# Depthwise convolution of the RG-LRU branch moved into the projections of an S5 / RG-LRU layer on Trainium2

## The chip, the cores and the metric

The kernel runs on one core of one Trainium2 chip. The core has five engines: TensorE (PE, with its weight loads shown as PEld), VectorE (DVE), ScalarE (ACT), GpSimd (POOL) and SyncE (SP, which only issues transfers here). The metric is the device time in microseconds; lower is better. Times of this kernel are medians of repeated executions; the profile is of one execution.

## The reference

One layer of a hybrid backbone, sequence 2048, width 1024, with 256 context tokens in front. All is float32.

```python
z = (rmsnorm(h) * (1 + sc) + sh) @ w_in                  # 1024 -> 4096, tokens and context
u_s5, g_s5, u_lru, g_lru = split(z)                      # 1024 columns each
y_s5  = s5_branch(u_s5, ...)                             # bidirectional state space scan, GLU
xc    = centred_dwconv(u_lru, conv_w) + conv_b           # 4 taps, pad (1, 2), per channel, along time
r, gi = sigmoid(blockdiag(w_a) xc + b_a), sigmoid(blockdiag(w_x) xc + b_x)   # 16 heads of 64, 2 directions
a     = exp(-8 r softplus(-lam));  bx = sqrt(1 - a^2) * (gi * xc)
h     = scan(a, bx)                                      # forward and backward, started from the context's end
out   = rmsnorm(h_in + gate * (concat(y_s5 * silu(g_s5), y_lru * silu(g_lru)) @ w_out))
```

The convolution is depthwise: each channel is the weighted sum of four neighbouring time steps of itself plus a bias. Context and tokens are convolved apart from each other.

## The kernel before

Channels lie on the 128 partitions and time on the free axis. The 1024 channels of a kind are eight blocks of 128, a block of u_lru being one pair of heads. Tokens are four tiles of 512 (0 to 3); the context is one tile of 256 ("c"). Float32 products are made as three passes of a rounded format (`mm3`, L248 to L250, high and low parts), so a tile of 512 columns with a contraction of 1024 takes 24 matmuls.

`projections(half, kinds)` computes a half of the sequence at a time: half 0 has "c", tiles 0 and 1, half 1 has tiles 2 and 3. It is a generator with eight steps a tile. For each block it splits the weights (L240 on ACT, L241 on DVE; half 1 reads split weights back from DRAM at L267), runs the matmuls into one of four PSUM tiles, and evacuates. A u_lru tile is copied by ACT (L313) into a staging tile with two buffers, `st2`, and stored on ACT's queue (L315) to a DRAM tensor `U`; a g_lru tile is activated and stored to `GL`. In half 0 the order is all u_lru blocks, all u_s5, all g_lru, all g_s5, except that the first two u_lru blocks are taken as [c, 0], [c, 0], [1], [1], since tile 1 of the normalised input is still being made.

Beside half 0 runs a side generator, `prepare`, at 0.1375 steps for each projection step: the tables of the S5 branch (`s5_tables`: products on DVE at L602 to L604, transposes on PE at L634, stores on POOL), then the input tiles 2 and 3.

`lru` is a generator beside half 1. On PE the order is the program's (`manual_schedule`, L1112); on the other engines a planner orders by program position among what it thinks ready. For each head pair b it runs `gates` (ten groups of eight small 64x64 matmuls at L397 with one projection step behind each group; half of them read `xc`, half read `xs`, the same data with the two heads exchanged), ACT's sigmoids (L401), then 34 more projection steps during which ACT does tanh, exp and sqrt (L444, L451, L459), DVE multiplies `gi` by `xc` (L447), and the next pair is prepared: `load(b + 1)` reads `U` into `ut` on SP's queue (L372, L373), `conv` makes `xc` with one ACT instruction (L378) and three of DVE (L381) over 2307 columns, and two DMAs on POOL's queue (L385) make `xs`. `ut` and `xs` share one buffer, `xc` has one. `finish(b)` (L407 to L423) does the scans and the product with `GL` on DVE beside the gates of pair b + 1, and stores `YL` on POOL's queue. The first call of `lru` comes after 32 steps of half 1, its first gates 28 steps later.

## Time and profile before

| what | value |
|---|---|
| time, median of 3 runs | 1915.83 us (1912.74 to 1917.07) |
| the profiled execution | 1915.55 us, of which the span is 1913.8 us |
| PE busy | 1728.6 us, 90% of the span |
| DVE / ACT / POOL busy | 1163.8 / 871.7 / 133.1 us |
| mean granted TensorE clock | 0.955 |
| idle of PE before the 259-column gates that read `xs` | 57.4 us |

Matmul records overlap, so PE's busy time says where it idles and not how fast it goes. The granted clock is a share of full speed and stands beside each stretch. The profiled execution agrees with the median within 0.3 us.

The stages of the span are: preparation to 56 us; half 0 from 56 to 544 (u_lru to 213, u_s5 to 344, then g_lru and g_s5); half 1 from 544, with the gates of the eight head pairs from 592 to 1001; then the rest of half 1, the S5 branch, the gated unit and the output projection.

### The profile page before, as it was taken

The numbers are of one execution on the slowest core, as the hardware profiler recorded it, in microseconds if no ns is written. First come the engines' busy times: TensorE is split into PE (matmuls) and PEld (weight loads), VectorE is DVE, ScalarE is ACT, GpSimd is POOL, SyncE is SP. The second block draws the span as 40 slices with busy tenths as digits, with TensorE's granted clock in tenths as the row PEclk, the third lists the DMA queues.
The fourth block names the chain that finished last, engine by engine and source line by source line (L and its number), as shares of the span: only waits on it lengthen the run. The fifth ranks groups of instructions, "written<-read, shape, count | busy, mean of one in ns | idle before, by whom it ended". The sixth has DMA issues, their size and how long they took to land.

```text
span 1913.8 us, 25929 instructions
## 1 busy us (share of the span) xinstructions
PE 1728.6 (90%) x9785; PEld 1370.3 (72%) x9785; DVE 1163.8 (61%) x1950; ACT 871.7 (46%) x1359; POOL 133.1 (7%) x260
## 2 busy tenths in 40 slices
PE   7889999999997887988788996987889999999998
PEld 2676888777874555554456885766878899998886
DVE  5789998741232767576777058999921046435563
ACT  2622232233633666765565887315545534222221
POOL 1012221210000000000000000000000000001111
PEclk9899999999998889998899998998999999999999
DMA  8677787865463456455557877426688766656653
GB/s 264 165 205 267 254 269 227 273 246 166 123 242 121 145 168 195 140 167 178 144 149 218 255 249 231 146 67 201 209 240 264 215 199 197 180 156 204 199 187 86
DMA packets 340207, 373.58 MB, mean 195 GB/s; under 512 B 124413, under 2 KB 276593, under 8 KB 327794
## 3 DMA queue, kind: packets, MB, share of 16 engines
q1 hardware_dynamic: 288176, 233.99, 42.5%
q0 software_dynamic: 19776, 94.92, 14.0%
q10 hardware_dynamic: 32130, 43.01, 6.5%
q8 instruction: 77, 1.26, 0.3%
q14 instruction: 48, 0.39, 0.1%
HBM read 224.05 MB, written 138.35 MB: 189 GB/s over the span
## 4 chain that ended last, share of the span: by engine, by line
PE 57%; DVE 17%; DMA 12%; issue 8%; ACT 4%; SPq 1%; POOL 0%; ACTq 0%; DVEq 0%; POOLq 0%
PE pp L248 9%; PE pp L250 8%; PE pp L249 8%; DVE p L748 4%; PE po L248 4%; PE po L250 4%; PE po L249 4%; PE pg L397 3%; PE pgl L249 3%; PE pgl L248 3%; PE pgl L250 3%; DVE z L749 3%; DVE z L750 3%; DMA xs<-xc 2%; DVE xc L381 2%
## 5 line engine op out<-in xcount | busy, mean ns | idle before, releaser
L248 PE MATMUL pp<-x,w 128*128 128x512 f32 x1024 | 424.2, 414 | 2.1 <-ACT ust L313 2.1
L250 PE MATMUL pp<-x,w 128*128 128x512 f32 x1024 | 407.7, 398 | 2.7 <-DVE w L241 2.7
L249 PE MATMUL pp<-x,w 128*128 128x512 f32 x1024 | 408.0, 398 | 0.2 <-DVE x L213 0.2
L248 PEld LDWEIGHTS pp<-x,w 128*128 128x128 f32 x1024 | 194.4, 190 | 112.1 <-issue 73.2
L250 PEld LDWEIGHTS pp<-x,w 128*128 128x128 f32 x1024 | 194.8, 190 | 47.9 <-DVE w L241 3.5
L249 PEld LDWEIGHTS pp<-x,w 128*128 128x128 f32 x1024 | 195.3, 191 | 36.6 <-issue 0.7
L241 DVE TENSOR_TENSOR w<-wraw,w 128x1024 fp32r<-128x1024 f32 x66 | 80.7, 1222 | 165.2 <-ACT w L240 165.2
L397 PE MATMUL pg<-xs,gw 64*64 64x512 f32 (+1 forms) x320 | 105.0, 646 | 58.4 <-DMA xs<-xc 45.9
L240 ACT CAST w<-wraw 128x1024 fp32r<-128x1024 f32 x66 | 69.2, 1048 | 155.8 <-PE pp L250 123.6
L783 PE MATMUL py<-h,et 128*128 128x128 f32 x512 | 82.4, 286 | 34.9 <-ACT h L776 16.9
L397 PE MATMUL pg<-xc,gw 64*64 64x512 f32 (+1 forms) x320 | 103.1, 636 | 7.9 <-issue 7.3
L250 PE MATMUL po<-x,w 128*128 128x512 f32 x256 | 101.9, 398 | 9.1 <-DVE w L241 9.1
L748 DVE TENSOR_TENSOR p<-z,A 128x128 f32<-128x128 f32 x288 | 104.3, 381 | 5.7
L248 PE MATMUL po<-x,w 128*128 128x512 f32 x256 | 105.4, 412 | 1.0 <-ACT z L727 0.6
L720 PE MATMUL pw<-u,wt 128*128 128x144 f32 x512 | 76.6, 298 | 29.2 <-DMA wt<-WD 21.7
L249 PE MATMUL po<-x,w 128*128 128x512 f32 x256 | 101.7, 397 | 0.7 <-DVE x L814 0.7
L401 ACT ACTIVATE rr<-pg,vcol 128x512 f32<-128x512 f32 (+1 forms) x80 | 51.7, 646 | 106.3 <-PE pg L397 106.3
L248 PE MATMUL po<-ws,yh 128*128 128x512 f32 x256 | 99.6, 389 | 0.0
L249 PE MATMUL po<-ws,yh 128*128 128x512 f32 x256 | 99.6, 389 | 0.0
L250 PE MATMUL po<-ws,yl 128*128 128x512 f32 x256 | 99.6, 389 | 0.0
L720 PEld LDWEIGHTS pw<-u,wt 128*128 128x128 f32 x512 | 72.4, 198 | 37.3 <-ACT z L727 14.5
L783 PEld LDWEIGHTS py<-h,et 128*128 128x128 f32 x512 | 71.0, 201 | 37.2 <-ACT h L776 19.0
(256 smaller groups left out, 3549.0 us busy)
## 6 DMA issues: line engine op xcount, KB each, us to landing
wraw<-in_w_in_dram SPq DMA_DIRECT2D x50, 512.0 KB
WS<-w POOLq DMA_DIRECT2D x24, 1024.0 KB, 7.3
w<-WS SPq DMA_DIRECT2D x24, 1024.0 KB
u<-ZU SPq DMA_DIRECT2D x64, 288.0 KB
ED<-E POOLq DMA_DIRECT2D x16, 1024.0 KB, 6.3
WD<-Wt POOLq DMA_DIRECT2D x32, 512.0 KB, 4.9
wt<-WD SPq DMA_DIRECT2D x32, 512.0 KB
et<-ED SPq DMA_DIRECT2D x32, 512.0 KB
```

The costliest lines, as they stand in the source:

```text
L240: copy(out=w[:, 0], in_=raw)
L241: self.nc.vector.tensor_sub(out=w[:, 1], in0=raw, in1=w[:, 0])
L248: nc.tensor.matmul(ps, lhsT=whi(k), rhs=xhi(k), start=(k == 0), stop=False)
L249: nc.tensor.matmul(ps, lhsT=whi(k), rhs=xlo(k), start=False, stop=False)
L250: nc.tensor.matmul(ps, lhsT=wlo(k), rhs=xhi(k), start=False, stop=(k == KT - 1))
L397: nc.tensor.matmul(pss[w][e * 64:e * 64 + 64, :n], lhsT=gw[ws, d, e, :], rhs=xcs[(w + e) % 2][ws, o:o + n], start=True, stop=True, tile_po ...
L401: nc.scalar.activation(out=dst[:, o:o + n], in_=pss[w][:, :n], func=AF.Sigmoid, bias=bias[w])
L720: nc.tensor.matmul(pw[:, c, :], lhsT=w[:, gi, kt, c, :], rhs=u[:, kt, :], start=(kt == 0), stop=(kt == 1))
L748: v.tensor_mul(out=p, in0=cur.unsqueeze(1).to_broadcast([P, 2, 2, 32]), in1=self.A16[:, :, :, gs])
L749: v.tensor_add(out=nxt, in0=nxt, in1=p[:, 0])
L750: v.tensor_add(out=nxt, in0=nxt, in1=p[:, 1, ::-1])
L783: nc.tensor.matmul(o, lhsT=ms(e[:, i, gi]), rhs=h[:, i, :], start=False, stop=(i == 1))
```

## The change

The convolution leaves `lru` and is done in `projections`, once for the context and once for each half of the tokens. A u_lru tile is copied into a buffer `u` (one buffer, tag `uc`, pool `ucp`) with the padding columns beside it. After tile "c" and after the last tile of the block, `conv` runs one ACT instruction and three of DVE on it into `xcv` (one buffer) and stores the result on POOL's queue into the DRAM tensor `XC`, which takes the place of `U`. Half 0 leaves out the last two columns that need tokens of half 1 and keeps three columns in `halo`; half 1 takes them up, so it convolves 1026 columns, half 0 256 and 1022.

In `lru`, `load` reads `XC` three times on SP's queue: the two 64-row halves into `xs` exchanged, and all rows into `xc`. `xs` and `xc` have a buffer each, and the gate weights `gw` one instead of two. Weights and data of pair b + 1 are asked for after exp in the program, not before tanh. The first four blocks of half 0 are now u_lru [c, 0], g_lru [0], u_lru [1], g_lru [1] of block 0, and the two weight blocks loaded ahead are those.

```diff
--- before.py
+++ after.py
@@ projections @@
         if half == 0:
-            kind, n = kinds[0][0], int(2)
-            blocks[:n] = [(kind, b, ["c", 0]) for b in range(n)] + [(kind, b, [1]) for b in range(n)]
+            blocks.remove(("g_lru", 0, both))
+            blocks[:1] = [("u_lru", 0, ["c", 0]), ("g_lru", 0, [0]), ("u_lru", 0, [1]), ("g_lru", 0, [1])]
...
+            if kind == "u_lru" and tiles[0] != 1:
+                u = self.conv_input(half, b)
...
-                if kind in ("u_lru", "g_lru"):
+                if kind == "u_lru":
+                    pos = 1 if tl == "c" else (3 if half else LC + 4) + tl % 2 * 512
+                    nc.scalar.copy(out=u[:, pos:pos + n], in_=ps[:, :n])
+                    if tl == "c":
+                        self.conv(half, b, u, 0)
+                elif kind == "g_lru":
                     o = self.stp.tile([P, 512], F32, tag="st2", bufs=2, name="ust")
-                    if kind == "u_lru":
-                        nc.scalar.copy(out=o[:, :n], in_=ps[:, :n])
-                        pos = 0 if tl == "c" else LC + tl * 512
-                        nc.scalar.dma_start(out=self.U[r, pos:pos + n], in_=o[:, :n])
...
+            if kind == "u_lru" and tiles[-1] == both[-1]:
+                self.conv(half, b, u)
...
+    def conv_input(self, half, b):
+        nc = self.nc
+        if half == 0:
+            u = self.ucp.tile([P, LC + 4 + 1024], F32, tag="uc", bufs=1, name="uc")
+            nc.gpsimd.memset(u[:, 0:1], 0.0)
+            nc.gpsimd.memset(u[:, LC + 1:LC + 4], 0.0)
+        else:
+            u = self.ucp.tile([P, 1024 + 5], F32, tag="uc", bufs=1, name="uc")
+            nc.gpsimd.memset(u[:, 1027:1029], 0.0)
+            nc.scalar.copy(out=u[:, 0:3], in_=self.halo[:, b, :])
+        return u
+
+    def conv(self, half, b, u, part=1):
+        nc = self.nc
+        cw, cb = self.col["lru_conv_w"], self.col["lru_conv_b"]
+        r = slice(b * P, (b + 1) * P)
+        if half:
+            o, dst, N = 0, LC + 1022, 1026
+        else:
+            o, dst, N = ((0, 0, LC), (LC + 3, LC, 1022))[part]
+        xc = self.ucp.tile([P, 1026 if half else 1024], F32, tag="xcv", bufs=1, name="xcv")[:, :N]
+        nc.scalar.activation(out=xc, in_=u[:, o + 1:o + 1 + N], func=AF.Identity, bias=cb[:, b:b + 1],
+                             scale=cw[:, 8 + b:9 + b])
+        for k in (0, 2, 3):
+            nc.vector.scalar_tensor_tensor(out=xc, in0=u[:, o + k:o + k + N], scalar=cw[:, k * 8 + b:k * 8 + b + 1],
+                                           in1=xc, op0=ALU.mult, op1=ALU.add)
+        nc.gpsimd.dma_start(out=self.XC[r, dst:dst + N], in_=xc)
+        if part and not half:
+            nc.vector.tensor_copy(out=self.halo[:, b, :], in_=u[:, LC + 1025:LC + 1028])
@@ lru @@
-        X0 = LC + 3
-        N = X0 + L
+        N = LC + L
...
-            gw = le.tile([P, 2, 2, 64], F32, tag="gw", bufs=2, name="gw")
+            gw = le.tile([P, 2, 2, 64], F32, tag="gw", bufs=1, name="gw")
...
         def load(b):
-            ut = le.tile([P, N + 3], F32, tag="ut", bufs=1, name="ut")
-            nc.gpsimd.memset(ut[:, 0:1], 0.0)
-            nc.gpsimd.memset(ut[:, LC + 1:LC + 4], 0.0)
-            nc.gpsimd.memset(ut[:, N + 1:N + 3], 0.0)
-            nc.sync.dma_start(out=ut[:, 1:1 + LC], in_=self.U[rows(b), 0:LC])
-            nc.sync.dma_start(out=ut[:, X0 + 1:X0 + 1 + L], in_=self.U[rows(b), LC:])
-            return ut
-
-        def conv(b, ut):
+            xs = big("xs", 1, le)
+            for e in range(2):
+                o = b * P + 64 - e * 64
+                nc.sync.dma_start(out=xs[e * 64:e * 64 + 64, :], in_=self.XC[o:o + 64, :])
             xc = big("xc", 1, le)
-            nc.scalar.activation(out=xc, in_=ut[:, 1:1 + N], func=AF.Identity, bias=cb[:, b:b + 1],
-                                 scale=cw[:, 8 + b:9 + b])
-            for k in (0, 2, 3):
-                v.scalar_tensor_tensor(out=xc, in0=ut[:, k:k + N], scalar=cw[:, k * 8 + b:k * 8 + b + 1],
-                                       in1=xc, op0=ALU.mult, op1=ALU.add)
-            xs = le.tile([P, N + 3], F32, tag="ut", bufs=1, name="xs")
-            for e in range(2):
-                nc.gpsimd.dma_start(out=xs[e * 64:e * 64 + 64, :N], in_=xc[64 - e * 64:128 - e * 64, :])
+            nc.sync.dma_start(out=xc, in_=self.XC[rows(b), :])
             return xc, xs
...
-            if b < 7:
-                gw2, ut = weights(b + 1), load(b + 1)
             for d in range(2):
...
             if b < 7:
-                gw, xcs = gw2, conv(b + 1, ut)
+                gw, xcs = weights(b + 1), load(b + 1)
@@ build @@
-            self.U = dt("U", [D, LC + L])
+            self.XC = dt("XC", [D, LC + L])
...
+                    self.halo = cp.tile([P, 8, 3], F32, name="halo")
                     xa = pool(eA, "xa")
+                    self.ucp = pool(eA, "ucp")
...
-                            self.first = [self.wload(win[:, :, 2 * D + b * P:2 * D + (b + 1) * P]) for b in range(2)]
+                            self.first = [self.wload(win[:, :, k * D:k * D + P]) for k in (2, 3)]
...
                     lru = self.lru(pool(eL, "lp"), pool(eL, "le"))
+                    self.ucp = pool(eL, "ucp1")
```

## Rows read from the trace of the kernel before

**Rows 1.** Windows by stage; the first line names the columns.

```profile
core 0: us, PE busy (x) PEld busy (x) DVE busy (x) ACT busy (x) POOL busy (x), PEclk, DMA share, GB/s
56.40:100.40 44.00, 41.20 (x232) 34.25 (x233) 35.17 (x61) 26.61 (x43) 5.01 (x4) 0.96 0.64 173
100.40:124.00 23.60, 18.29 (x106) 13.43 (x106) 16.47 (x15) 2.60 (x4) 1.08 (x2) 0.86 0.95 219
124.00:213.40 89.40, 86.56 (x570) 67.67 (x569) 85.64 (x112) 25.41 (x48) 22.77 (x33) 1.00 0.67 238
...
280.00:344.10 64.10, 64.10 (x428) 53.13 (x427) 50.95 (x65) 17.32 (x34) 12.72 (x22) 1.00 0.80 237
344.10:410.00 65.90, 65.90 (x390) 52.39 (x389) 50.26 (x64) 20.99 (x35) 13.32 (x23) 1.00 0.75 265
...
592.20:1001.50 409.30, 346.91 (x1592) 200.24 (x1592) 273.32 (x120) 260.80 (x279) 13.27 (x44) 0.89 0.51 154
```

**Rows 2.** Groups, 560 to 1010: xcount, busy us, mean ns, idle before.

```profile
L381 DVE SCALAR_TENSOR_TENSOR xc<-ut,vcol,xc 128x2307 f32<-128x2307 f32 x24 | 62.9, 2620 | 48.7 <-ACT xc L378 48.0
...
L378 ACT ACTIVATE xc<-ut,vcol 128x2307 f32<-128x2307 f32 x8 | 18.5, 2313 | 2.0 <-DMA ut<-U 1.4 <-DMA gw<-in_lru_w_a_dram 0.6
...
L397 PE MATMUL pg<-xs,gw 64*64 64x259 f32 x64 | 22.3, 517 | 57.4 <-DMA xs<-xc 45.9 <-issue 11.5
```

**Rows 3.** PE's timeline: start, us; before the first gates, last gates.

```profile
587.85 0.39 PE L250 MATMUL pp<-x,w 128*128 128x512 f32 x1
...
1000.89 0.59 PE L397 MATMUL pg<-xc,gw 64*64 64x512 f32 x1
```

**Rows 4.** PE's timeline: last gate of pair 0, gates of pair 1.

```profile
620.11 0.59 PE L397 MATMUL pg<-xc,gw 64*64 64x512 f32 x1
...
644.65 0.65 PE L397 MATMUL pg<-xc,gw 64*64 64x259 f32 x2
...
649.17 1.12 PE L397 MATMUL pg<-xs,gw 64*64 64x259 f32 x2 [3.88 <-DMA xs<-xc]
...
658.07 0.64 PE L397 MATMUL pg<-xc,gw 64*64 64x512 f32 x1
...
672.83 0.59 PE L397 MATMUL pg<-xc,gw 64*64 64x512 f32 x1
```

**Rows 5.** Windows of 10 us, gates of pair 1 (columns above).

```profile
650.00:660.00 10.00, 7.83 (x32) 2.82 (x31) 9.93 (x5) 3.03 (x6) 0.00 (x0) 0.63 0.25 72
```

**Rows 6.** Timelines of DVE and POOL between gates of pairs 0, 1.

```profile
624.28 2.56 DVE L447 TENSOR_TENSOR gi<-gi,xc 128x2307 f32<-128x2307 f32 x1 [8.79 <-ACT gi L401]
...
633.09 5.35 DVE L381 SCALAR_TENSOR_TENSOR xc<-ut,vcol,xc 128x2307 f32<-128x2307 f32 x2 [6.25 <-ACT xc L378]
...
644.08 1.02 POOL L385 DMA_DIRECT2D xs<-xc  x2 [23.11 <-DMA w<-WS]
```

**Rows 7.** DMA issues: xcount, KB each, median us to landing.

```profile
WD<-Wt POOLq DMA_DIRECT2D x32, 512.0 KB, 4.9
...
xs<-xc POOLq DMA_DIRECT2D x16, 576.8 KB, 6.9
...
YL<-rr POOLq DMA_DIRECT2D x8, 1024.0 KB, 6.4
...
out_dram<-ot POOLq DMA_DIRECT2D x60, 128.0 KB, 4.7
```

**Rows 8.** Groups: 124 to 213.4, and (last line) 560 to 1010.

```profile
L604 DVE TENSOR_TENSOR E<-E,ot 128x1024 f32<-128x1024 f32 x10 | 12.2, 1219 | 0.0
...
L248 PE MATMUL pp<-x,w 128*128 128x512 f32 x80 | 32.4, 405 | 0.0
...
L167 DVE SCALAR_TENSOR_TENSOR gacc<-wgt,cond,gacc 128x1024 f32<-128x1024 f32 x3 | 3.9, 1285 | 4.9 <-DMA wgt<-in_w_mod_dram 4.8
```

**Rows 9.** SP's waits, 560 to 1010: us in total, times, longest.

```profile
SPq L267 <- PE pp L250: 165.1, 21, 28.4
SPq L420 <- DVE tt L414: 110.9, 6, 22.9
```

More of the change, by code (lines that the diff above doesn't have):

```diff
@@ L309, in projections @@
                         yield
-                if kind in ("u_lru", "g_lru"):
+                if kind == "u_lru":
[4 more added lines that the diff above has]
+                elif kind == "g_lru":
                     o = self.stp.tile([P, 512], F32, tag="st2", bufs=2, name="ust")
-                    if kind == "u_lru":
-                        nc.scalar.copy(out=o[:, :n], in_=ps[:, :n])
-                        pos = 0 if tl == "c" else LC + tl * 512
-                        nc.scalar.dma_start(out=self.U[r, pos:pos + n], in_=o[:, :n])
-                    else:
-                        if half:
-                            nc.scalar.activation(out=o, in_=ps, func=AF.Sigmoid)
-                            nc.vector.tensor_mul(out=o, in0=ps, in1=o)
-                        else:
-                            nc.scalar.activation(out=o, in_=ps, func=AF.Silu)
-                        nc.scalar.dma_start(out=self.GL[r, tl * 512:tl * 512 + 512], in_=o)
+                    if half:
+                        nc.scalar.activation(out=o, in_=ps, func=AF.Sigmoid)
+                        nc.vector.tensor_mul(out=o, in0=ps, in1=o)
+                    else:
+                        nc.scalar.activation(out=o, in_=ps, func=AF.Silu)
+                    nc.scalar.dma_start(out=self.GL[r, tl * 512:tl * 512 + 512], in_=o)
                 elif kind == "u_s5":
@@ L344, in projections @@
                     nc.sync.dma_start(out=self.ZU[kt, r, :, cs], in_=st[:, kt * 8:kt * 8 + 8, :])
+    def conv_input(self, half, b):
[13 more added lines that the diff above has]
+        r = slice(b * P, (b + 1) * P)
+        if half:
+            o, dst, N = 0, LC + 1022, 1026
[10 more added lines that the diff above has]
+            nc.vector.tensor_copy(out=self.halo[:, b, :], in_=u[:, LC + 1025:LC + 1028])
     def lru(self, lp, le):
         nc, v = self.nc, self.nc.vector
-        X0 = LC + 3
-        N = X0 + L
-        tl_x = [(X0 + i * 512, 512) for i in range(4)]
-        cw, cb = self.col["lru_conv_w"], self.col["lru_conv_b"]
-        c_, x_ = slice(0, LC), slice(X0, N)
+        N = LC + L
+        tl_x = [(LC + i * 512, 512) for i in range(4)]
+        c_, x_ = slice(0, LC), slice(LC, N)
         rows = lambda b: slice(b * P, (b + 1) * P)
@@ L391, in gates @@
             bias = [self.col[n][:, d * 8 + b:d * 8 + b + 1] for n in ("lru_b_a", "lru_b_x")]
-            for o, n in [(0, X0)] + (tl_x if d == 0 else tl_x[::-1]):
+            for o, n in [(0, LC)] + (tl_x if d == 0 else tl_x[::-1]):
                 pss = [pool.tile([P, 512], F32, tag=tag, name="pg") for pool, tag in ((self.psG, "g"), (self.psT, "t"))]
@@ L426, in lru @@
         gw = weights(0)
-        xcs = conv(0, load(0))
+        xcs = load(0)
         yield 28
```

## Prediction

> **What bounds the kernel now.** I read three views in this order: the busy shares by stage, the waits of TensorE in the stage that the change is about, and then DVE in the stage that gets the new work.
>
> By stage, PE is busy without a break in the later part of half 0, where it alone sets the time. Two stretches are different [rows 1]. From 592 to 1001 us, the gates of the eight head pairs, PE is busy 347 of 409 us at a granted clock of 0.89: this is the worst stretch of the first half. From 124 to 213 us, the u_lru blocks of half 0, PE is busy 86.6 of 89.4 us, but DVE is busy 85.6: there the two are nearly level, and DVE has no room.
>
> In the gates the chain of one pair can be followed [rows 4, 6]. The last gate of pair 0 ends at 620.7 (620.11 + 0.59). PE then runs 34 projection steps until the first gate of pair 1 at 644.65, which is 23.95 us. The gates that read `xs` start only at 649.17, after an idle time that ended with the DMA from `xc` to `xs`. That DMA was issued at 644.08, because the convolution stands before it: DVE's first two products started at 633.09. Over all pairs PE idles 57.4 us before the short gates that read `xs`, most of it for that DMA [rows 2]. The idle time costs twice: between 650 and 660 the granted clock is 0.63, so part of the stretch ran at the lower level (1.2 GHz instead of 2.4), right after PE had idled [rows 5]. The first gates of pair 1 took 1.12 us for a pair of 259 columns; later ones take 0.64 us for 512 columns [rows 4].
>
> **Part by part: the gates.** Removed per pair are one ACT instruction of 2.31 us and three of DVE of 2.62 us [rows 2], and the transfer of `xs` behind them. What is left of the chain is a load. Its parts, after the gates end at G: `gw` and `xs` may be issued at G, since their buffers come free then; `xc` may be issued when the second product L447 has read the old one. In pair 0 that is 624.28 + 2.56 = 626.8, or G + 6.1 [rows 6]. No row shows these reads, so I bound them by the nearest ones: one transfer of 1024 KB took 6.4 us and one of 577 KB 6.9 us [rows 7]. If the three overlap, `xc` ends last, at G + 6.1 + 6.4 = G + 12.5. If they follow each other, it is 6.9 + 6.9 + 6.4 = 20.2, so G + 20.2. PE arrives at G + 23.95. Both ends are ahead of it, so I let the wait vanish, with a margin of 3.8 to 11.5 us.
>
> The row of 577 KB has 64 partitions a transfer, the one of 1024 KB has 128; per byte the first is about half as fast. The Trainium skill, in "SBUF — State Buffer", section "Door 1: The DMA port swizzle", says that 64 partitions in a row reach only half of the ports, and further on that two such transfers do not add up. The rows agree with the first. By that rule the later bound, G + 20.2, would be the true one, and the margin would be 3.8 us; it speaks against loading the exchanged halves apart.
>
> What would the gates then take? From 658.07 the eight groups of pair 1 that follow the wait end at 673.42 (672.83 + 0.59), which is 15.35 us or 1.92 us a group [rows 4]. Ten groups are 19.2 us. Today the stretch from the end of the projections before the first gates (587.85 + 0.39 = 588.24) to the last gate (1000.89 + 0.59 = 1001.48) is 413.2 us [rows 3]. Without waits and at full clock it is 8 x 19.2 + 7 x 23.95 = 321.3 us. The most that can be gained is 91.9 us. I take off 2 us a pair, 16 us in all, for what comes late next: half of the 3.9 us for which PE waited at the gates of pair 1 [rows 4]. What will be late is ACT, which must evacuate both gate tiles between tanh, exp and sqrt, or a weight block whose load stands behind a waiting entry of SP's queue; SP already waits up to 28.4 us there [rows 9]. So the gates give 76 us, bounds 46 (below) and 91.9.
>
> Behind them DVE is the next engine. It is busy 273 us in this stretch [rows 1]; 24 products of 2307 columns, 63 us, go [rows 2], and 24 of 1026, priced below, come. The pitch of a pair falls from about 52 to 45 us, and DVE then has (273 - 63 + 31) / 8 = 30 us of work in it. It does not become the bound.
>
> **Half 0.** The same work over fewer columns comes here. A DVE product of this kind costs 1.285 us over 1024 columns [rows 8] and 2.62 over 2307 [rows 2], so 1.04 ns a column and 0.22 us fixed: 1.29 us for 1022 or 1026 columns and 0.49 for 256. A block is 3 x 1.29 + 3 x 0.49 plus a small copy for `halo`, about 5.5 us, of DVE; 8 x 3 x 1.29 = 31 us is what half 1 gets. ACT's part is 1.0 us per 1000 columns (2.31 for 2307), some 1.3 us a block; ACT is busy 25 of 89 us there and hides it. DVE does not. Before 124 us it has 8.8 + 7.1 = 15.9 us idle [rows 1], which take the 11 us of blocks 0 and 1. Blocks 2 to 7 bring 33 us into a stretch with 3.8 us idle, so 29 us must push something: the S5 tables or PE. If the tables slide, they find 13.2 + 15.6 us idle between 280 and 410 [rows 1], and the cost is nothing. If they go first, PE waits: a u_lru tile can't be copied into `u` before the convolution of the block before has read it, and behind that copy on ACT stand the weight casts and the table copies. PE has four PSUM tiles to run ahead, about one block. A block now takes 89.4 / 5 = 17.9 us (80 records of L248 are five blocks of two tiles and eight steps [rows 8]). So I charge 29 - 17.9 = 11 us, bounds 0 and 29.
>
> The new stores go to POOL's queue, behind the table stores, 16 in half 0. One of 512 KB took 4.9 us, one of 128 KB 4.7 [rows 7]. `xcv` has one buffer, so there is a ring for each block: 1.1 + 3.9 + 4.9 for the long part and 0.4 + 1.5 + 4.7 for the context, 16.5 us. That is under 17.9, so it costs nothing as long as DVE serves it at once. The 40 stores of `U` on ACT's queue go. The bytes written stay; 19 MB are read from DRAM where 9.5 were read and 9.5 copied.
>
> **The start.** The second u_lru block's tile "c" no longer fills the time in which tile 1 of the input is made. That tile is 256 of a block's 1280 columns, so at most a fifth of 17.9 us, 3.6 us; with the 1.5 us of DVE work that now stands ahead of the input's own I charge 4 us, bounds 0 and 5. The early silu and the extra pads on POOL I cost at nothing: they lie beside PE.
>
> **Sum.** The profiled execution took 1915.6 us, 0.2 under the median. 1915.6 - 76 + 11 + 4 = 1855 us (1854.6).
>
> **The rivals.** (1) The ring decides, and the kernel gets slower. If each of the two parts of a block's convolution must wait for two triples of table products on DVE (6 x 1.22 = 7.3 us [rows 8]), the ring is 16.5 + 14.6 = 31.1 us instead of 17.9, and PE follows it over seven blocks: 92 us. 1915.6 - 76 + 92 + 4 = 1936 us. It decides from 17.9 + 72 / 7 = 28 us a block on. For it speaks DVE at 96% there; against it, that convolution steps are early in the program compared with the tables that follow. (2) The loads come too late, one wait for another: SP's queue is in order, a load of `GL` waits up to 22.9 us in it and weight loads up to 28.4 [rows 9], and the loads are now asked for after exp. If that takes half of the 91.9 us, it is 1915.6 - 46 + 15 = 1885 us. The rule on 64 partitions named above would bring this about with 4 us of delay instead of 11. (3) Half 0 and the start hide everything and nothing comes late: 1915.6 - 91.9 = 1824 us. (4) The change doesn't do what it says, if PE's order at the gates was set by ACT anyway and not by `xs`: then nothing is gained and 15 us are lost, 1931 us. The gap of 3.88 us that ends with the DMA [rows 4] speaks against it.
>
> **How the numbers follow.** The forecast has 0.52, rival 1 0.12, rival 2 0.18, rival 3 0.14, rival 4 0.04. A measurement of this kernel tells about 0.2% (4 us) from no change. Faster by more: the forecast, rivals 2 and 3 but 0.03 of them that ends near zero or above, so 0.81. Slower: rivals 1 and 4, and 0.01 of rival 2, so 0.17. That leaves 0.02 for the same. The range goes from 1822, just under rival 3, to 1908, which takes in rival 2 with 23 us for a wait that eats more than half; rivals 1 and 4 are left out.
>
> **What would show it.** In the profile after: the gates of a pair last 19 to 21 us and follow at a pitch near 45; no idle time of PE ends with a DMA into `xs` or `xc`; the granted clock of the stretch is near 1. The u_lru blocks of half 0 take 18 to 20 us; if they take 28 or more, rival 1 holds. If PE's gates end their idle time with a DMA from `XC`, or PE's projections with one from `WS`, rival 2 holds. The prediction is wrong if the gain of the gates is given back later, where DVE or the S5 branch waits.

## The result and the profile after

| what | before | after |
|---|---|---|
| time, median of 4 runs each | 1916.26 us (1912.74 to 1917.07) | 1861.32 us (1854.51 to 1868.49) |
| ratio, with its 95% interval | | 0.9717 (0.9677 to 0.9757) |
| the profiled execution: time, span | 1915.55, 1913.8 us | 1854.51, 1852.7 us |
| mean granted TensorE clock | 0.955 | 0.967 |

The kernel is 55 us faster; the prediction was 1855 us, with a range of 1822 to 1908. The profiled execution of after is the fastest of its four, so its trace shows some 61 us where the medians show 55.

The first view is the windows by stage of the kernel after: the u_lru blocks 2 to 7 of half 0, its u_s5 blocks, its g blocks, half 1 up to the first gates, and the gates. The columns are those of [rows 1].

```profile
core 0: us, PE busy (x) PEld busy (x) DVE busy (x) ACT busy (x) POOL busy (x), PEclk, DMA share, GB/s
109.10:244.50 135.40, 114.01 (x681) 90.20 (x680) 125.58 (x171) 39.41 (x68) 32.56 (x61) 0.90 0.55 199
244.50:381.10 136.60, 133.94 (x906) 109.38 (x905) 129.89 (x169) 40.28 (x76) 30.46 (x55) 1.00 0.83 254
381.10:566.60 185.50, 185.50 (x978) 149.88 (x977) 62.67 (x83) 84.81 (x130) 16.24 (x28) 1.00 0.58 189
566.60:618.30 51.70, 43.02 (x186) 34.31 (x184) 20.75 (x19) 8.80 (x14) 1.42 (x5) 0.96 0.72 244
618.30:943.90 325.60, 322.44 (x1592) 193.33 (x1592) 241.00 (x117) 250.47 (x282) 7.46 (x18) 0.97 0.61 191
```

The last line answers the last line of [rows 1]: the same 1592 matmuls from the first gate to the last took 409.3 us and take 325.6, with PE busy for 322.4 of them, and the granted clock is 0.97 where it was 0.89. The second view is PE's timeline at the gates of pair 1; it answers [rows 4].

```profile
663.06 0.43 PE L422 MATMUL pg<-xc,gw 64*64 64x256 f32 x1
663.07 0.43 PE L422 MATMUL pg<-xs,gw 64*64 64x256 f32 x2
...
681.21 0.59 PE L422 MATMUL pg<-xc,gw 64*64 64x512 f32 x1
```

The gates that read `xs` start 0.01 us after those that read `xc`, and the pair takes 18.7 us (663.06 to 681.80). Over all eight pairs the groups of PE's instructions, 615 to 945 us, show what is left of the waits; the columns are those of [rows 2].

```profile
L422 PE MATMUL pg<-xc,gw 64*64 64x512 f32 (+1 forms) x320 | 92.2, 595 | 8.5 <-DMA GL<-ust 8.0 <-ACT rr L426 0.5
L422 PE MATMUL pg<-xs,gw 64*64 64x512 f32 (+1 forms) x320 | 91.0, 594 | 2.7 <-ACT gi L426 2.7
```

Before, 57.4 us of idle time stood before the short gates on `xs` alone [rows 2]; now 11.2 us stand before all gates, and 8.0 of these are one wait, before the first pair.

The third part is the ledger between the two profiled executions, cut at the same instructions. The last projection matmul before the first gates ends at 588.24 us before [rows 3] and at 610.27 after (609.88 + 0.39, below): +22.0 us. From there to the end of the last gate it is 413.2 us before and 333.7 after (943.35 + 0.59 = 943.94): -79.5. From the last gate to the end of the span it is 912.3 and 908.8: -3.5. The sum is -61.0, the difference of the spans 61.1. So half 0 lost 22 us and the gates won 80.

Where half 0 lost them is shown by the waits of ACT, 54 to 250 us (us in total, times, longest), and the landing of the new stores (size, median us).

```profile
ACT xcv L376 <- DMA XC<-xcv: 33.1, 8, 12.1
...
ACT uc L314 <- DVE halo L383: 24.6, 3, 16.9
```

```profile
XC<-xcv POOLq DMA_DIRECT2D x8, 511.0 KB, 6.4
XC<-xcv POOLq DMA_DIRECT2D x8, 128.0 KB, 2.1
```

ACT can't begin a convolution until the store of the one before has left `xcv`, and can't copy the next block's tile out of PSUM until DVE has read the one `uc`. The largest of PE's own waits there, in the same view, end with that copy; the others end with work of DVE's:

```profile
PE pp L248 <- ACT uc L314: 13.5, 4, 6.0
PE psk L673 <- DVE halo L383: 3.9, 1, 3.9
PE psw L657 <- DVE W L627: 3.4, 2, 2.8
```

Last, the longest wait that is left in the gates. These are rows of ACT's, POOL's, SP's and PE's timelines of the kernel after, from 591 to 618 us.

```profile
591.94 0.48 ACTq L175 DMA_DIRECT2D GT<-gt  x1
594.50 0.19 ACT L362 COPY uc<-halo 128x3 f32<-128x3 f32 x1 [5.35 <-DMA GT<-gt]
...
601.29 0.56 POOL L381 DMA_DIRECT2D XC<-xcv  x1 [6.48 <-ACT uc L362]
...
604.50 1.12 SPq L408 DMA_DIRECT2D xs<-XC  x2
605.67 0.58 SPq L410 DMA_DIRECT2D xc<-XC  x1
...
609.88 0.39 PE L250 MATMUL pp<-x,w 128*128 128x512 f32 x1
618.27 0.66 PE L422 MATMUL pg<-xc,gw 64*64 64x256 f32 x1 [8.01 <-DMA GL<-ust]
```

Half 1's first `uc` waits for the store of `GT`, the row of the output gate that the side work computes last, because the two share memory at different times. That delays the convolution, its store to `XC`, the loads, and the first gates. The page names a store of `GL` at the end of the 8.01 us; the loads that the gates read were issued 12 to 14 us earlier, and I take it that these ended the wait (the page puts a wait for several down to one). That a transfer ended it fits the windows: from 610.27 to 618.27 us the DMA share is 0.90, from there to 624 it is 0.00; which transfer it was is not shown.

### The profile page after: what moved, and what is told of

The parts are those of the page before. It is cut to its first block, busy times and chain, and to the rows that moved or that the text cites. A ratio compares the mean times of both kernels' runs of the same rounds, so it can differ in the third digit from the quotient of the medians.

```text
span 1852.7 us, 25971 instructions
## 1 busy us (share of the span) xinstructions
PE 1714.9 (93%) x9785; PEld 1372.4 (74%) x9785; DVE 1165.6 (63%) x2006; ACT 875.1 (47%) x1382; POOL 138.4 (7%) x268
## 3 DMA queue, kind: packets, MB, share of 16 engines
q1 hardware_dynamic: 288304, 243.43, 45.8%
## 4 chain that ended last, share of the span: by engine, by line
PE 51%; issue 17%; DVE 16%; DMA 10%; ACT 4%; SPq 1%; POOL 1%; ACTq 0%; DVEq 0%; POOLq 0%
PE pp L248 7%; PE pp L249 7%; PE pp L250 7%; PE po L250 4%; PE po L248 4%; PE po L249 4%; DVE p L771 4%; PE pgl L250 3%; PE pgl L248 3%; PE pgl L249 3%; DVE z L772 3%; DVE z L773 3%; DMA YT<-y 2%; PE pw L743 2%; PE pg L422 1%
## 5 line engine op out<-in xcount | busy, mean ns | idle before, releaser
L248 PE MATMUL pp<-x,w 128*128 128x512 f32 x1024 | 422.9, 413 | 14.0 <-ACT uc L314 13.5
L422 PE MATMUL pg<-xc,gw 64*64 64x512 f32 (+1 forms) x320 | 92.2, 595 | 8.5 <-DMA GL<-ust 8.0
L422 PE MATMUL pg<-xs,gw 64*64 64x512 f32 (+1 forms) x320 | 91.0, 594 | 2.7 <-ACT gi L426 2.7
L379 DVE SCALAR_TENSOR_TENSOR xcv<-uc,vcol,xcv 128x256 f32<-128x256 f32 (+2 forms) x72 | 73.0, 1014 | 22.0 <-ACT xcv L376 21.3
```

The source lines that it names most:

```text
L248: nc.tensor.matmul(ps, lhsT=whi(k), rhs=xhi(k), start=(k == 0), stop=False)
L379: nc.vector.scalar_tensor_tensor(out=xc, in0=u[:, o + k:o + k + N], scalar=cw[:, k * 8 + b:k * 8 + b + 1], in1=xc, op0=ALU.mult, op1=ALU.add)
L422: nc.tensor.matmul(pss[w][e * 64:e * 64 + 64, :n], lhsT=gw[ws, d, e, :], rhs=xcs[(w + e) % 2][ws, o:o + n], start=True, stop=True, tile_po ...
```

## The experiments

The theory was: the gates gained because DVE's taps and the exchange on chip no longer stand between two pairs; half 0 lost because DVE got 31 us of new work in the blocks where it was nearly full. Rivals for the gates: ACT set the order, or it was the loads and not the taps. Rivals for half 0: the new block order, or the single buffers `uc` and `xcv` (rival 1 of the prediction in a smaller form). Ratios below are to the kernel before, run on the same chip. A difference to after is of medians; where the two ratios give another one, it stands in brackets behind.

**Experiment 1: the kernel before without the taps.**

```diff
-            for k in (0, 2, 3):
+            for k in ():
                 v.scalar_tensor_tensor(out=xc, in0=ut[:, k:k + N], ...
```

> The kernel before, with the three VectorE taps of the depthwise convolution left out in the RG-LRU stage (the ScalarE first tap, the exchange on chip and everything else stay; so the convolution is not computed in full). My theory: the gates of a pair wait for xs at the end of a chain (convolution on VectorE, then the exchange by DMA); three taps of 2.62 us each are 7.9 us of that chain, and the waits before xs shrink by as much where they are that long: the stretch of the gates falls from 413 us towards 340 to 360, the time by 50 to 75 us to about 1840 to 1865. Rival (ScalarE sets the order of the pairs, xs is only the wait that ends last): the waits at xs move to another releaser and the time falls by less than 10 us.

Measured: 1843.58 us, ratio 0.9632 (0.9610 to 0.9653), 70 us under before. The window of its gates, and the group that [rows 2] shows with 57.4 us of idle time:

```profile
587.20:929.40 342.20, 326.10 (x1593) 193.85 (x1592) 219.49 (x99) 259.70 (x279) 12.27 (x42) 0.97 0.60 184
...
L397 PE MATMUL pg<-xs,gw 64*64 64x512 f32 x256 | 82.1, 652 | 7.9 <-ACT gi L401 7.9
...
L397 PE MATMUL pg<-xs,gw 64*64 64x259 f32 x64 | 12.4, 404 | 4.4 <-DMA xs<-xc 3.6 <-PE pg L397 0.8
```

With ACT's part, the transfer on chip and everything else in place, the wait for `xs` falls from 45.9 to 3.6 us and the stretch from 409.3 to 342.2. The same 259-column gates take 404 ns in the mean instead of 517: the granted clock is 0.97 instead of 0.89. ACT did not set the order; rival 4 of the prediction falls. What is left to wait for is ACT: 7.9 us before the long gates on `xs`.

**Experiment 2: the kernel before with the new block order.**

```diff
-            kind, n = kinds[0][0], int(2)
-            blocks[:n] = [(kind, b, ["c", 0]) for b in range(n)] + [(kind, b, [1]) for b in range(n)]
+            blocks.remove(("g_lru", 0, both))
+            blocks[:1] = [("u_lru", 0, ["c", 0]), ("g_lru", 0, [0]), ("u_lru", 0, [1]), ("g_lru", 0, [1])]
```

(and the first two weight blocks as in the kernel after)

> The kernel before, with only the new order of the first two projection blocks of half 0 and the new pair of first weights (the convolution stays in the RG-LRU stage). My theory: +4 us (0 to 5), since the second block's weights and split come at another place in front of the first tiles. Rival: the order is the larger part of the 22 us that half 0 lost, +10 to +22.

Measured: 1914.99 us, ratio 1.0004 (0.9991 to 1.0017). Half 1 starts 1.6 us later than in before (545.90 against 544.34 in PE's timelines). The order costs nothing that can be measured. This kernel has the block order of after and no convolution in half 0, so its windows of the same blocks are what after's two first windows are to be held against:

```profile
109.50:227.10 117.60, 106.05 (x681) 82.82 (x680) 108.48 (x138) 29.80 (x56) 26.34 (x39) 0.94 0.65 232
227.10:358.90 131.80, 131.80 (x905) 109.06 (x904) 115.63 (x151) 37.77 (x72) 28.45 (x50) 1.00 0.85 255
```

DVE went from 224.1 us in 249.4 to 255.5 in 272.0: 31.4 us more work and 22.6 us more time.

**Experiment 3: the kernel after without the taps of half 0.**

```diff
-        for k in (0, 2, 3):
+        for k in (0, 2, 3) if half else ():
             nc.vector.scalar_tensor_tensor(out=xc, in0=u[:, o + k:o + k + N], ...
```

> The kernel after, with the three VectorE taps left out in half 0 alone (so the convolution is not computed in full there); buffers, first tap, stores and order stay. Theory A (VectorE work beside the table products is what half 0 lost): 13 to 22 us faster than the kernel after, about 1840 to 1848. Theory B (the single buffers, the stores and their landing): 0 to 6 us faster than the kernel after. Theory C (the order of the blocks): no change.

Measured: 1828.30 us, ratio 0.9550 (0.9525 to 0.9575), 33 us under after; by the profiled executions 25.7. The windows of the same blocks:

```profile
110.90:230.00 119.10, 107.86 (x682) 84.69 (x681) 109.42 (x144) 40.11 (x68) 32.11 (x62) 0.94 0.64 228
230.00:361.20 131.20, 131.20 (x905) 109.08 (x904) 116.07 (x152) 38.92 (x73) 29.33 (x51) 1.00 0.86 259
```

250.3 us, within 1 us of experiment 2: the copies into `uc`, ACT's part, the stores and the rings of single buffers cost nothing by themselves. All that half 0 lost needs the taps. Theory A's 13 to 22 us were exceeded, but only in part by half 0: by the profiled executions 19.3 us lie ahead of the first gate (599.02 against 618.27), 3.1 in the gates and 3.3 behind them; the medians differ by more because after's profiled execution was its fastest. The run doesn't yet say why: a tap is DVE time, and it is also what holds `uc` and `xcv`.

**Experiment 4: half 1's convolution buffers in other memory.**

```diff
+                    self.ucp = pool(eL, "ucp1")
                     lru = self.lru(pool(eL, "lp"), pool(eL, "le"))
-                    self.ucp = pool(eL, "ucp1")
```

> The kernel after, with the pool of half 1's convolution opened before the RG-LRU pools, so that its buffer lies elsewhere and does not wait for the store of GT. My theory: the one wait left in the gates (8.0 us before the first pair, which begins with half 1's first convolution waiting 5.4 us for that store) goes: 8 to 11 us faster than the kernel after, about 1851. Rival: the first pair's loads are late in any case (the queue or the transfer of 12.6 us), 0 to 3 us.

Measured: 1865.19 us, ratio 0.9752 (0.9723 to 0.9781): no gain (7 us over after by the ratios). The wait that it was made for did go: from half 1's first matmul to the first gate it is 43.3 us (571.9 to 615.2) instead of 51.7. But a new one came after the gates. Its PE waits, 600 to 1000 us, and SP's, 930 to 1000:

```profile
PE pw L743 <- DMA wt<-WD: 20.6, 1, 20.6
...
SPq L759 <- DMA YL<-rr: 6.1, 1, 6.1
```

And the first load of the S5 branch on SP's timeline, in after and then here:

```profile
950.23 1.42 SPq L759 DMA_DIRECT2D u<-ZU  x2
950.98 32.83 SPq L234 DMA_DIRECT2D wraw<-in_w_in_dram  x6
990.17 0.92 SPq L759 DMA_DIRECT2D u<-ZU  x2
```

Opening the pool first moves every buffer of the RG-LRU stage. The loads of the S5 branch now stand behind six loads of weights in SP's queue, so its first `u` tile is asked for 40 us later than in after, and the first table `wt` behind it. The last step before it is the wait of 6.1 us for the store to `YL`, which I take to be a buffer that the new `u` tile now shares; after waits 6.9 us at the same load, for DVE, so this wait alone is not the reason. Why the planner puts the weights first here is not shown. From the last gate to the end it is 922.8 us instead of 908.8. The theory of the wait holds, the expectation of the time does not.

**Experiment 5: the kernel after with the heads exchanged on chip.**

```diff
-            xs = big("xs", 1, le)
-            for e in range(2):
-                o = b * P + 64 - e * 64
-                nc.sync.dma_start(out=xs[e * 64:e * 64 + 64, :], in_=self.XC[o:o + 64, :])
             xc = big("xc", 1, le)
             nc.sync.dma_start(out=xc, in_=self.XC[rows(b), :])
+            xs = big("xs", 1, le)
+            for e in range(2):
+                nc.gpsimd.dma_start(out=xs[e * 64:e * 64 + 64, :], in_=xc[64 - e * 64:128 - e * 64, :])
```

> The kernel after, with xs made on chip again: xc alone is loaded from XC and the heads are exchanged from xc to xs by the two GpSimd-issued transfers of the kernel before. My theory (what cost the gates their time was VectorE's taps in the chain, not where the exchange is done): the chain is the load of xc, about 6 us for one 1.18 MB transfer, and then the exchange, 6.4 to 6.9 us as before, which still ends before the next gates, 24 us after the last: 0 to +10 us on the kernel after. Rival (the plain loads from DRAM are what takes the wait away): the wait before xs returns in most of the eight pairs, 3 us a pair or more, +20 to +60.

Measured: 1867.28 us, ratio 0.9771 (0.9752 to 0.9789), 6 us over after (10 by the ratios). The window of the gates and PE's waits, 615 to 962 us:

```profile
618.90:959.30 340.40, 325.50 (x1592) 193.79 (x1592) 241.92 (x118) 250.75 (x283) 16.65 (x36) 0.97 0.60 188
...
PE pg L421 <- DMA xs<-xc: 6.8, 3, 4.5
PE pg L421 <- DMA xc<-XC: 4.0, 1, 4.0
PE pg L421 <- ACT gi L425: 3.3, 7, 1.3
PE pg L421 <- ACT rr L425: 3.2, 2, 2.8
```

The stretch is 340.4 us, 15 more than after, as long as that of experiment 1 (342.2) in which the taps alone were taken out. Two experiments from opposite sides agree on the taps: of the 83.7 us between 409.3 and 325.6, 67 to 69 come from their leaving the chain. The other 15 to 17 go with the exchange through DRAM, but only about half of them can be seen to be its own: 8 of the 15 are the first pair (28.7 us against 20.8), which holds all but 0.2 of the 6.8 us that PE waits for `xs`. The rest stands in pairs whose waits end with ACT or with no releaser that the profile shows. In the time of the whole kernel the 15 us are a few only, at the edge of the two intervals.

**Experiment 6: the taps ahead of the table products.**

```diff
+        with (ExitStack() if half else self.tc.high_priority(offset=250)):
             nc.scalar.activation(out=xc, ...
             (the taps and the store, as they are)
```

> The kernel after, with the convolution of half 0 raised in the scheduler's order, so that its VectorE taps stand ahead of the table products emitted before them; the work is the same. Theory A (VectorE is full from 109 to 245 us, 125.6 of 135.4, so order gives nothing back): -5 to +5 us on the kernel after, with TensorE's waits moving from ScalarE's copies into uc to the table products. Theory B (TensorE waits because the taps stand behind table products; the amount of work is no matter): 10 to 20 us faster than the kernel after.

Measured: 1855.90 us, ratio 0.9714 (0.9695 to 0.9732): the same as after. PE's waits, 54 to 250 us:

```profile
PE pp L248 <- ACT uc L314: 8.1, 5, 2.7
PE psk L674 <- DVE BR L608: 6.5, 1, 6.5
PE psw L658 <- DVE W L628: 6.0, 3, 3.0
```

The waits for the copy into `uc` fall from 13.5 to 8.1 us, and those for table products rise from 4.0 (3.4 for `W`, 0.6 for `BI`) to 12.5, with 3.3 more for the table `kk`. Blocks 2 to 7 with the u_s5 blocks take 271.8 us, as in after (272.0). Order only says who waits. This is what a full DVE would do; experiment 7 shows that DVE is not all of it.

**Experiment 7: buffers of its own for the context part.**

```diff
-            u = self.ucp.tile([P, LC + 4 + 1024], F32, tag="uc", bufs=1, name="uc")
+            u = self.ucp.tile([P, 1 + 1024], F32, tag="uc", bufs=1, name="uc")
+            self.uctx = self.ucp.tile([P, LC + 3], F32, tag="ux", bufs=1, name="ux")
...
+        (the context's result goes to a tile of the staging ring st2, the x part's stays in xcv)
```

> The kernel after, with buffers of its own for the context part of half 0's convolution (its u, and its result in another ring), so that the context's taps and its store no longer hold the one uc and the one xcv of a block. Theory A (VectorE is full): 0 to 5 us faster than the kernel after. Theory B (rival 1 of the prediction in a small form: the ring of single buffers makes TensorE wait, 13.5 us before copies into uc on the page): 8 to 14 us faster.

Measured: 1845.68 us, ratio 0.9663 (0.9643 to 0.9683), 16 us under after (10 by the ratios). The windows of the same blocks, and ACT's waits, 54 to 250 us:

```profile
110.20:231.70 121.50, 108.48 (x673) 84.97 (x672) 116.55 (x156) 38.93 (x66) 30.56 (x62) 0.94 0.58 209
231.70:369.30 137.60, 136.80 (x914) 109.62 (x914) 134.31 (x180) 40.44 (x76) 33.10 (x59) 1.00 0.85 257
...
ACT xcv L379 <- DMA XC<-xcv: 15.1, 6, 7.9
```

The same work takes 259.1 us instead of 272.0, and DVE is busy for 250.9 of them, 97%. ACT's wait for the store out of `xcv` is 15.1 us instead of 33.1. So theory B is right for about half of the loss: the context's store and taps held the buffers of the x part. This execution is the fastest of its four by 7 us; experiment 12, with the same buffers, has 261.1 us for the same work. What is left over experiment 2 is 10 to 12 us, with DVE nearly always busy.

**Experiment 8: fewer table products in the u_lru blocks.**

```diff
-    merge(self.projections(0, ...), [side, 0.1375])
+    p0 = self.projections(0, ...)
+    for n, rate in ((192, 0.11), (192, 0.1375), (256, 0.17)):
+        merge(islice(p0, n), [side, rate])
```

> The kernel after, with the side work of half 0 (the S5 tables and what follows them) handed out at another rate: 0.11 steps a K-step in the u_lru blocks instead of 0.1375, 0.1375 in the u_s5 blocks, 0.17 in the g blocks, where VectorE is busy for 62 of 185 us. The work is the same, 90 steps. Theory A (VectorE is full in the u_lru blocks): about 5 of 26 steps leave them, at some 3.5 us of VectorE work each, so half 0 is 13 to 20 us shorter, and the row of the gate is done earlier, which shortens the one wait left in the gates by up to 5: 13 to 22 us faster than the kernel after. Theory B (order and buffers): 0 to 5 us.

Measured: 1858.74 us, ratio 0.9728 (0.9710 to 0.9746): the same as after. The windows of the same blocks, and the row of ACT's timeline on which the first gates hang:

```profile
110.80:244.30 133.50, 111.51 (x659) 88.39 (x658) 119.26 (x160) 36.47 (x63) 30.31 (x57) 0.92 0.54 195
244.30:374.70 130.40, 130.40 (x880) 108.22 (x879) 116.48 (x151) 39.89 (x73) 27.25 (x49) 1.00 0.84 247
...
603.32 0.19 ACT L362 COPY uc<-halo 128x3 f32<-128x3 f32 x1 [17.60 <-DMA GT<-gt]
```

Taking 6 us of DVE work out of the u_lru blocks made them 2 us shorter: with the shared buffers, they seem to go by the ring and not by DVE's load. The u_s5 blocks are 6 us shorter. Then it is given back: the side work ends later, `GT` is stored later, and half 1's first `uc` waits 17.6 us for it instead of 5.4; the first gate comes at 624.6 instead of 618.3. Both parts of my expectation (13 to 20 us in half 0, an earlier `GT`) were wrong.

**Experiment 9: two buffers for the x part as well.**

```diff
-            u = self.ucp.tile([P, 1 + 1024], F32, tag="uc", bufs=1, name="uc")
+            u = self.ucp.tile([P, 1 + 1024], F32, tag="uc", bufs=2, name="uc")
...
+            xc = self.stp.tile([P, T, 64], F32, tag="st4", bufs=1, name="xcv")     (x part of half 0)
```

> The kernel with the context's own buffers (e7), and two buffers for the x part's u in place of one, with its result in the st4 buffer that lies idle until the u_s5 blocks, so that a block's first x tile is copied out of PSUM while the block before is still in its taps. Theory B (what half 0 still loses against the kernel before is the wait for the one uc): half 0 ends 5 to 11 us earlier than in e7, at 545 to 551 us of the trace, and the time is 5 to 10 us under e7's 1846. Theory A (VectorE is full): 0 to 3 us, with TensorE waiting for the table products instead.

Measured: 1850.84 us, ratio 0.9674 (0.9651 to 0.9698), not under experiment 7. The windows of the same blocks, and two of PE's waits in experiment 2:

```profile
113.70:223.10 109.40, 102.84 (x634) 82.52 (x633) 105.47 (x140) 34.60 (x59) 27.68 (x55) 0.97 0.60 216
223.10:378.90 155.80, 147.48 (x953) 115.18 (x952) 143.70 (x194) 43.26 (x82) 35.66 (x64) 0.97 0.77 237
...
PE psk L650 <- DVE BR L584: 7.3, 1, 7.3
PE psk L650 <- DVE BI L587: 2.3, 1, 2.3
```

The six u_lru blocks take 109.4 us, 12 less than in experiment 7: PE no longer waits for a copy into `uc`. (They are also 8 shorter than in experiment 2, which has no convolution there, but that run waits 9.6 us in its window for two tables, where this one waits 1.5.) The u_s5 blocks take 155.8, 18 more than in experiment 7, with DVE busy for 143.7: PE ran ahead of the table products and then met them. Of its instructions 634 lie in the first window and 953 in the second, where after has 681 and 906. Together it is 265.2 us. DVE's work over the two stretches is 249 to 256 us in after and in experiments 6, 7 and 9, and no arrangement of buffers comes under it. The u_lru blocks did what the expectation said, the time did not: half 1 starts at 565.55 us, 9.5 later than in experiment 7, and the waits moved to the table products, as the rival had it.

**Experiment 10: the side work faster in the g blocks alone.**

```diff
+    merge(islice(p0, 384), [side, 0.1375])
+    merge(p0, [side, 0.18])
```

> The kernel after, with the side work handed out at 0.18 steps a K-step instead of 0.1375 in the g blocks of half 0 alone, so that it is emitted about 35 K-steps before half 0 ends. My theory (the 8.0 us before the first gates come from half 1's first uc, which lies over the memory of the gate's row and waits for the store of GT): GT is stored earlier, the wait goes, and nothing moves in memory: 8 to 11 us faster than the kernel after. Rival (the gate's row starts when the last x tile's buffers come free and goes by its weight loads, about 30 us whatever the emission): no change, 0 to 3 us.

(Step 384 comes two tiles before the end of the u_s5 blocks, since the two early tiles of g_lru stand before them.)

Measured: 1854.66 us, ratio 0.9694 (0.9678 to 0.9710), 7 us under after (4 by the ratios, whose intervals overlap). `GT` is stored some 10 us earlier, the 8.0 us before the first gates are gone, and in their place PE waits 2.9 us earlier, for the side work itself:

```profile
579.27 1.56 PE L172 MATMUL psg<-gacc,ones 128*128 128x512 f32 x3 [2.89 <-DVE gacc L167]
```

From half 1's first matmul to the first gate it is 45.8 us (572.1 to 617.9) instead of 51.7, and the first pair takes 17.8 us at a granted clock of 1.00, instead of 20.8 at 0.84 behind the wait of 8 us. The gain is a little under the 8 to 11 us that I expected; unlike in experiment 4 nothing moved in memory and nothing was given back later.

**Experiment 11: experiments 9 and 10 together.**

> e9 and e10 together. If the two add: the sum of their gains against the kernel after, 1828 to 1842. If the gate's row doesn't move with the rate: as e9.

Measured: 1845.88 us, ratio 0.9663 (0.9635 to 0.9691): 15 us under after (10 by the ratios), 5 under experiment 9. This is above the 1828 to 1842 that I had written for the case that the gains add; by the ratios the two alone give 8 and 4, so it is about their sum, and the range came from what I had expected of the two and not from what they gave. The first pair is at 17.8 us again, and the u_s5 blocks still last 156 us (219.7 to 376.1).

**Experiment 12: experiments 7 and 10 together.**

> e7 (the context's own buffers) and e10 (0.18 in the g blocks) together, one u buffer. If the two gains add, as they act on stretches that don't meet (u_lru blocks of half 0; the first gates): 1836 to 1842, which is under every kernel so far that computes the whole reference. If e7's gain is given back later as e9's was (its u_lru blocks were shorter by 8 us more than e7's, and its u_s5 blocks longer by 18): 1846 or more.

Measured: 1839.76 us, ratio 0.9626 (0.9613 to 0.9639). The gains add, and this is the fastest kernel that computes everything: 22 us under after (17 by the ratios), 70 under before. Its windows of the same blocks are those of experiment 7 (123.5 and 137.6 us), and its first gates come 50.1 us after half 1's start, behind a wait of 5.0 us for the row of the gate.

## Why the prediction was right, and where not

**The gates: right, in mechanism and in size.** Predicted -76 us, measured -79.5. The ideal was 321.3 us and 16 us of friction; it came to 333.7, so 12.4 of friction, of which 8.0 are one wait that I had not foreseen. The other 4.4 us are a sum over eight pairs where I took 2 us a pair. Nothing takes the place of the wait in pairs 1, 3, 4, 5, 6 and 7, whose gates last 18.4 to 18.9 us, a little under the ideal 19.2. Pair 0 takes 20.8 and pair 2 takes 24.9. All follow 24.0 us after the last ones (predicted 23.95). Pair 2 is the case that I had named for the friction, ACT late with a gate tile; here are the row of its wait, its window, and the window of the same pair in experiment 7.

```profile
717.14 0.68 PE L422 MATMUL pg<-xs,gw 64*64 64x256 f32 x1 [1.60 <-ACT gi L426]
...
705.76:730.68 24.92, 23.32 (x109) 8.26 (x108) 24.74 (x13) 13.88 (x22) 0.64 (x2) 0.79 0.27 99
...
694.75:716.87 22.12, 19.14 (x109) 6.87 (x108) 22.05 (x12) 13.69 (x22) 0.64 (x2) 1.00 0.26 98
```

The wait is 1.6 us, but the pair is 6.2 us longer than its neighbours, for the most part because the granted clock falls to 0.50 behind it. In experiment 7 PE waits there twice, 3.0 us in all, the clock stays at 1.00, and the pair takes 22.1. So the mechanism held, and that 16 us of friction came so near 12.4 is in part luck: most of it is a wait of another kind. Over the stretch the clock came back with the idle time, 0.97 after 0.89. Experiment 1 shows that the taps carry most of it; what goes with loading the exchanged heads from DRAM is at most about a sixth (experiment 5).

**The loads: in time, and earlier than the late bound.** For the first pair the two halves and the whole were issued between 604.50 and 606.25, and the gates that read all three start at 618.27: 13.8 us at most, where the late bound was made of three transfers one behind the other at the durations of [rows 7], 20.2 us. So they did not follow each other at those durations. The issue at G + 6.1 was too early a guess: in pairs 1 to 7 `xc` is asked for 7.4 to 15.0 us after the last gate. In the latest of these, pair 6, its gates still start without a wait 9.0 us after that (873.38 to 882.37). The Trainium skill, in "SBUF — State Buffer", section "Can I just issue two DMAs to hit both halves?", says that two concurrent transfers, one on a tile at partition 0 and one on a tile at partition 64, serialize. No run here isolates the two halves, so that is neither shown nor refuted; what was wrong was my making 20.2 us of it. Nor do the two rows of [rows 7] that the prediction held against the rule on 64 partitions settle it: in the same rows 512 KB took 4.9 us and 128 KB 4.7, so these durations don't go by bytes. Rival 2 fell: over the eight pairs no wait of PE but the first ends with a load, and that one is late because the convolution before it was.

**Half 0: the term that was mis-sized.** Predicted +11 and +4 for the start, measured +22.0. The start is 1.6 us by experiment 2, inside its 0 to 5. The taps are 22.6 us by the windows of after against experiment 2 (the g blocks give some 1.5 back). A u_lru block takes 22.6 us where I had written 18 to 20. The step that failed is the credit of one block, 17.9 us, for PE's running ahead in its four PSUM tiles. DVE's new work was right, 31.4 us measured where I had 33, but only 8.8 us of it were absorbed (31.4 less 22.6), where I had let 3.8 us of DVE's idle time and the 17.9 absorb 21.7. The sum also had a slip: the stretch from 124 to 213 us holds five blocks, 3 to 7, as its own 80 records say, and I set the work of six against it. Done rightly, the same method would have charged 27.5 - 3.8 - 17.9, about 6 us, instead of 11, further from what was measured. That so little was absorbed has two reasons, and the runs separate them. The four PSUM tiles don't help when the next block's first tile can't be copied out, because its buffer is still being read: that is the ring, and giving the context its own buffers brings back 11 to 13 us (272.0 to 259.1, and 261.1 in experiment 12). The other part is DVE's time: at 259.1 us it is 97% busy, and when PE is let go still further (experiment 9) it meets the table products, and its u_s5 blocks are 18 us longer. I had written that the tables would find idle time behind 280 us at no cost; DVE's work in the u_s5 blocks rose by 14 us (129.9 against 115.6, some 2 of it late taps), and this cost 4.8 us there.

**Rival 1** had the right mechanism with too high a price: the ring of the single buffers does decide the u_lru blocks of half 0 (experiments 7 and 8), but a block takes 22.6 us (135.4 / 6), not 31. The point from which the kernel would have been slower, 28 us, was not near.

**What was overlooked** is the one wait before the first gates. It comes from a fact that stood in the diff and not in a row: the new pool `ucp1` is opened last, over memory that the gate's row leaves last. It cost 8.0 us of waiting and some 3 us of low clock in the first pair. Experiment 10, in which it is gone, is 4 to 7 us under after; that gain is not clear of the noise by itself, but experiment 12 lies clear of experiment 7 by the same change.

**The sum.** 1915.6 + 22.0 - 79.5 - 3.5 = 1854.6 us, which is the profiled execution and the predicted 1855 to the microsecond; that is luck, two errors that cancel: 7 us too little charged in half 0 and 7 too little won in the gates and after them. The median is 7 us above the profiled execution. In experiments 4, 5 and 10, whose half 0 is that of after up to its g blocks, half 1 starts at 572 instead of 566.6, so the loss of half 0 is more often 27 than 22. The 3.5 us after the gates were not looked into.

## What to carry to other kernels

Work that is moved out of a chain of dependent steps is paid for where it lands: add its busy time to the engine's window there, and if the window was already above 90%, count on most of it (here 22.6 of 31.4 us). Do not credit run-ahead buffers (PSUM tiles here) unless the buffer behind them is free as well; the smallest part of the work (the context's 256 columns) can hold the largest buffer, and splitting the buffers was the repair that gave most here. A buffer opened over memory of an unrelated earlier stage takes on that stage's last store as a dependency, and moving it shifts every other buffer into new ones: read the first use of every new pool in the timeline, and what else moved. When a total agrees with a forecast, look at its parts one by one: here six pairs came in under the ideal, two over it, and a wait that the forecast did not have made up the rest.

## What the runs showed of the hardware that I had not expected

The low clock outlasts a wait: after the 8.0 us of idle time the granted clock is 0.50 from 618.27 to 624 us, which is the lower level of 1.2 GHz. The second and third groups of gates start 2.9 and 3.5 us after the one before them, instead of 1.5 and 1.9 us in experiment 10, and the pair takes 20.8 us instead of 17.8. A short wait can be enough: in pair 2, behind 1.6 us of idle time, the clock is 0.50 from 717 to 724 us. The same wait in experiments 3, 4 and 7 left the clock of the pair at 1.00, so it is not the wait alone, and what else decides is not shown.

In half 0 many short waits, none over 6.0 us, went with a granted clock of 0.90 over 135 us, where experiment 2 had 0.94 and experiment 9 0.97. What this cost is not shown: experiment 6 had 0.94 for the same blocks and took 135.1 us, as long as after with 0.90 (135.4).

A store to DRAM holds its source for longer than the work that made it: in the ring of `xcv` the three taps of the context take some 1.4 us (3 x 0.48), their store of 128 KB lands after 2.1 in the median and of the x part's 511 KB after 6.4, and ACT's longest wait for one was 12.1 us.
